# Mixed values, weight sums and weight splits re-ordered in the first, second and last u/gate group of a two-layer decoder trunk

## The chip, the cores and the metric

The kernel runs on one core of one Trainium2 chip, as one program. The metric is the device time of one execution in microseconds, the median of three timed runs. TensorE (PE in the profile) does the matrix products, VectorE (DVE) and ScalarE (ACT) work on what surrounds them, GpSimd (POOL) takes part of VectorE's kind of work, and SyncE (SP) issues the transfers between HBM and SBUF.

## The reference

One inference step of two layers on 1024 prompt tokens and 64 sample tokens, width 1024. Layer 0 is gated linear attention; layer 1, which the change touches, is a token-mixing MLP:

```python
def cmlp_mixer(h, w_in, ln_g, ln_b, w_spatial, b_spatial, w_out):
    u, v, gate = jnp.split(h @ w_in, 3, axis=-1)
    v = layernorm(v, ln_g, ln_b)
    ...
    mixed = jnp.einsum('gts,bnsgd->bntgd', ws, vg) + bs.T[:, :, None]
    z = u * mixed.reshape(bsz, t, CMLP_WIDTH) * jax.nn.silu(gate)
    return z @ w_out, v
```

Here `ws` is a 128x128 lower-triangular matrix for each of four groups of columns. A residual addition and a last RMSNorm follow. Everything is float32.

## The kernel before

**Arithmetic.** Each float32 operand of a product is written as a high part in the type float32r and a low part, the rest. A product is then three matmuls: high by high, high by low, low by high. Making the parts ("splitting") takes one ScalarE copy for the high part and one VectorE subtraction for the low part: `parts_of` (lines 969 to 974) and `fetch_w` (line 127 on ScalarE, line 128 on VectorE) for weights, `split` (lines 202 and 203) for activations.

**Stages.** Layer 0 comes first, then the projection to v (a block of 256 columns at a time, lines 1006 to 1050), then the u/gate stage that the change edits (the loop `for m in range(KT)`, eight groups m of 128 columns of u and 128 of gate), then the output projection `out_proj` with the weight blocks 28 to 31 (lines 790 to 862, matmuls at line 142).

**One u/gate group.** A group would be the product of a 256x1024 block of weights with 1088 tokens. It is done by a seven-product scheme of the Strassen kind on 2x2 quarters: seven quarter products (`product`, line 1004) with four sums of weight quarters, s1 to s4, three plain quarters, (1,1), (2,2) and (1,2), and sums of token quarters that were made beforehand (`tsum`). On TensorE a group is, in this order: the products with s2 (tile `pb`), s3 (`two`), s1 (`pb`), (1,1) (`p`); eight 128-column pairs of mixing matmuls (`mix`, line 1106); s4 (`pb`); the small mixing matmul of the 64 sample tokens (`mix`, line 1100); (2,2) (`two`); (1,2) (`p`). The mixing products go to two PSUM buffers (tag `o`). A chunk of four is taken out of its buffer by VectorE at line 1107, multiplied by a gain and added to `bias`, into `zt`; the small mixing matmul takes the first of the two buffers again, so it waits for the first instruction of line 1107.

**The weights of the next group.** `Quarters(blk)` loads a block's four pieces (256 KB each) into the single buffer `rawq` (line 964, on SyncE); `sums` makes s1 to s4 on GpSimd (line 985); `parts` splits a quarter or a sum (line 972 on ScalarE, 973 on VectorE) into a place whose old weights TensorE no longer needs. During group m the weights of group m+1 are summed and split, while `following` holds the load for group m+2, which can start when the last reader of `rawq` is done. The v rows of a group (`v_load`, tile `vm`) are loaded once the small mixing matmul of the group before has read them.

**Order.** The whole of the v and u/gate stages is written inside `in_order()`: on every engine the instructions run in the order of the code. An instruction that waits holds up everything behind it on its engine. After `order.close()` a scheduler chooses the order of the output projection again. The first group (m = 0) has its own placing of these steps, and so has the last (m = 7), since the operand `zs[0]` of the output projection (384 tokens of z: eight slices kt, of which 0 to 4 come through the tile `zstage`, 5 and 6 through two `zmore` tiles, 7 from `zt` directly) and the first weight block 28 (quarters 0 to 3, loaded by `load_w`, split by `fetch_w`) are split there.

**The tag `raw`.** The weight sums, the two `zmore` tiles and the loads of weight quarters take turns in three buffers; a load whose buffer still has a reader waits on SyncE, and so does all that is queued behind it there.

## Time and profile before

| | |
|---|---|
| timed runs | 940.91, 941.42, 944.12 us; median 941.42 us |
| the profiled execution | 944.72 us, of which 942.9 us from the first to the last instruction |
| mean granted TensorE clock | 0.991 |
| TensorE busy | 905.1 us, 96% of the span |
| VectorE, ScalarE, GpSimd busy | 640.8, 462.6, 285.4 us |
| u/gate groups m = 0 to 7 | from 637.71 us to 832.04 us of the span |
| output projection | from 832.04 us |

All places in time below are microseconds from the start of the span of this execution. A row of a timeline gives start, duration, engine, line, operation, output tile and input tiles, and how many instructions of one kind in a row it stands for; the bracket at its end is the idle time of the engine just before, and what ended it. A tile's name says which step a row belongs to: `wq` is a split weight, `qsum` a weight sum in a `raw` buffer, `qs` the sum s4, `half` a partial sum, `sg` the gate, `zt` the group's z, `act` the operand buffer, `wr` a loaded weight quarter of the blocks 28 to 31, `z` the later slices of the operand.

### The profile page before, as it was taken

The numbers are of one execution on the slowest core, as the hardware profiler recorded it, in microseconds if no ns is written. First come the engines' busy times: TensorE is split into PE (matmuls) and PEld (weight loads), VectorE is DVE, ScalarE is ACT, GpSimd is POOL, SyncE is SP. The second block draws the span as 40 slices with busy tenths as digits, with TensorE's granted clock in tenths as the row PEclk, the third lists the DMA queues.
The fourth block names the chain that finished last, engine by engine and source line by source line (L and its number), as shares of the span: only waits on it lengthen the run. The fifth ranks groups of instructions, "written<-read, shape, count | busy, mean of one in ns | idle before, by whom it ended". The sixth has DMA issues, their size and how long they took to land.

```text
span 942.9 us, 17092 instructions
## 1 busy us (share of the span) xinstructions
PE 905.1 (96%) x6437; PEld 880.3 (93%) x6437; DVE 640.8 (68%) x1288; ACT 462.6 (49%) x980; POOL 285.4 (30%) x307
## 2 busy tenths in 40 slices
PE   8989999999999999989999999999899999999995
PEld 8979989998999899978999999998899999999994
DVE  7888778677875877688553945556867777583246
ACT  7664544444462544554343644546444444455322
POOL 2023332232322331322133110023645555211123
PEclk9999999999999999999999999999989999999998
DMA  9302112311222112423574254463323332464133
GB/s 294 97 1 82 42 45 79 118 34 41 67 83 81 57 36 89 118 74 118 163 245 144 70 160 148 149 191 112 105 91 105 102 100 93 138 212 140 58 111 130
DMA packets 89967, 101.80 MB, mean 108 GB/s; under 512 B 9862, under 2 KB 80844, under 8 KB 89884
## 3 DMA queue, kind: packets, MB, share of 16 engines
q1 hardware_dynamic: 89884, 100.71, 34.0%
q8 instruction: 50, 0.82, 0.3%
q14 instruction: 33, 0.27, 0.1%
HBM read 74.26 MB, written 26.42 MB: 107 GB/s over the span
## 4 chain that ended last, share of the span: by engine, by line
PE 67%; DVE 14%; DMA 5%; issue 5%; ACT 5%; POOL 3%; SPq 1%; DVEq 0%; ACTq 0%; POOLq 0%
PE fm L142 28%; PE tm L156 12%; PE pb L1004 6%; PE two L1004 5%; PE p L1004 4%; DMA xsum<-x_spill 3%; PE sc L518 2%; PE pst L589 1%; PE o L628 1%; PE o L597 1%; DVE act L203 1%; DVE scT L531 1%; PE mix L1106 1%; PE first L285 1%; PE o L599 1%
## 5 line engine op out<-in xcount | busy, mean ns | idle before, releaser
L142 PE MATMUL fm<-act,w 128*128 128x384 f32 (+1 forms) x1632 | 290.2, 332 | 0.4 <-DVE act L203 0.4
L142 PEld LDWEIGHTS fm<-act,w 128*128 128x128 f32 x1632 | 269.8, 188 | 2.4 <-DVE act L203 0.6
L156 PE MATMUL tm<-w,act 128*128 128x256 f32 (+1 forms) x1536 | 192.6, 283 | 0.5 <-ACT vt L1015 0.5
L156 PEld LDWEIGHTS tm<-w,act 128*128 128x128 f32 x1536 | 185.4, 188 | 2.1 <-ACT vt L1015 0.7
L142 PE MATMUL fm<-act,wq 128*128 128x384 f32 (+1 forms) x576 | 96.6, 328 | 1.7 <-ACT wq L127 1.3
L142 PEld LDWEIGHTS fm<-act,wq 128*128 128x128 f32 x576 | 94.7, 188 | 3.2 <-ACT wq L127 1.6
L128 DVE TENSOR_TENSOR w<-wr,w 128x512 fp32r<-128x512 f32 (+1 forms) x80 | 57.3, 732 | 16.7 <-ACT w L127 16.1
L826 POOL TENSOR_TENSOR acc<-acc,sq 128x384 f32<-128x384 f32 (+1 forms) x30 | 31.0, 1037 | 110.0 <-ACT sq L821 109.5
L127 ACT ACTIVATE w<-wr 128x512 fp32r<-128x512 f32 (+1 forms) x80 | 48.7, 624 | 24.9 <-DMA wr<-w 13.2
L848 DVE TENSOR_TENSOR x<-fm,res 128x384 f32<-128x384 f32 (+1 forms) x40 | 21.0, 527 | 49.8 <-PE fm L142 49.8
L1004 PE MATMUL two<-tsum,wq 128*128 128x272 f32 x384 | 54.2, 299 | 0.1
L1004 PEld LDWEIGHTS two<-tsum,wq 128*128 128x128 f32 x384 | 51.7, 197 | 0.3 <-DVE wq L973 0.3
L821 ACT ACTIVATE sq<-x 128x384 f32<-128x384 f32 (+1 forms) x42 | 21.0, 503 | 62.1 <-DVE x L848 58.5
L1004 PE MATMUL pb<-act,wq 128*128 128x272 f32 x384 | 51.4, 290 | 0.0
L1004 PE MATMUL p<-act,wq 128*128 128x272 f32 x384 | 51.0, 288 | 0.0
L1004 PEld LDWEIGHTS p<-act,wq 128*128 128x128 f32 x384 | 49.4, 188 | 0.0
L1004 PEld LDWEIGHTS pb<-act,wq 128*128 128x128 f32 x384 | 49.0, 189 | 0.0
L473 POOL TENSOR_TENSOR xe<-xe,k 128x384 f32<-128x384 f32 (+2 forms) x24 | 28.7, 1197 | 44.2 <-ACT xe L472 41.1
L659 POOL TENSOR_TENSOR on<-on,g 128x384 f32<-128x384 f32 (+1 forms) x24 | 23.8, 1013 | 57.0 <-DVE on L658 34.2
L449 POOL TENSOR_TENSOR kd<-kd,k 128x384 f32<-128x384 f32 (+1 forms) x12 | 12.1, 1006 | 85.8 <-ACT kd L448 85.8
L973 DVE TENSOR_TENSOR wq<-qsum,wq 128x512 fp32r<-128x512 f32 x25 | 27.6, 1112 | 12.4 <-ACT wq L972 12.2
L480 DVE TENSOR_TENSOR xl<-cum 128x192 f32<-128x192 f32 (+4 forms) x72 | 35.1, 513 | 0.0
(265 smaller groups left out, 1641.8 us busy)
## 6 DMA issues: line engine op xcount, KB each, us to landing
wr<-w SPq DMA_DIRECT2D x92, 256.0 KB, 3.1
rawq<-w SPq DMA_DIRECT2D x32, 256.0 KB, 3.6
xsum<-x_spill SPq DMA_DIRECT2D x16, 272.0 KB, 3.3
z_spill<-zt SPq DMA_DIRECT2D x8, 544.0 KB, 2.8
s<-s SPq DMA_DIRECT2D x16, 256.0 KB, 3.9
state_s<-ns SPq DMA_DIRECT2D x32, 128.0 KB, 2.5
v_spill<-vt SPq DMA_DIRECT2D x32, 128.0 KB, 2.5
vm<-v_spill SPq DMA_DIRECT2D x8, 512.0 KB, 4.3
```

The source lines that it names most:

```text
L127: A.activation(w[:, 0], raw, AF.Copy)
L128: V.tensor_tensor(w[:, 1], raw, w[:, 0].bitcast(F32), ALU.subtract)
L142: PE.matmul(acc, lhs, rhs, start=(k == 0), stop=(k == 23))
L156: PE.matmul(acc, lhs, rhs, start=(k == 0), stop=(k == 23))
L473: G.tensor_tensor(xe, xe, kt_[:, :nl], ALU.mult)
L480: V.tensor_tensor(l3[:, :, lo:hi], c3[:, :, (i + 1) * m:], r, ALU.subtract)
L659: G.tensor_tensor(o, o, gate[h][:, j, t0:t0 + n], ALU.mult)
L821: A.activation(sq, raw[p][:, m, :], AF.Square)
L826: (V if gain is not None and p == 2 or m == KT - 1 else G).tensor_tensor(total, acc[p], sq, ALU.add)
L848: V.tensor_tensor(raw[p][:, m, :], pa, r, ALU.add)
L973: V.tensor_tensor(w[:, 1], src, w[:, 0].bitcast(F32), ALU.subtract)
L1004: PE.matmul(acc, lhs, rhs, start=start and k + i == 0, stop=k + i == 5, skip_group_check=not start)
```

## The change

Three places of the u/gate loop are written in another order; no work is added or left out. Line numbers move by up to 10 behind the first edit.

- First group (m = 0): the two line-1107 instructions go ahead of the three splits of plain quarters on VectorE; GpSimd makes the sums s3 and s4 right behind its four half-additions, ahead of its two multiplications into `zt`; the load of block 22 (`following`) is issued behind the three splits, ahead of the load of the next v rows on SyncE.
- Second group (m = 1): the two line-1107 instructions go ahead of the split of s3. In the groups 2 to 6 nothing changes.
- Last group (m = 7): slices 0 and 2 of the operand are split before the copies of the product with (1,1), slices 4 and 6 behind them; the loads of weight quarters 1 and 2 of block 28 are written sooner, quarter 1 is split behind the first SiLU instead of behind the second, quarter 2 behind the second; the two `zmore` buffers swap, so that the slice that is split first (6) holds the buffer that quarter 2 is loaded into.

The diff:

```diff
--- before.py
+++ after.py
@@ -1168,6 +1168,11 @@
             nxt.parts("s2", spare)
         if not more:
             fetch_w(28, [0])
+            load_w(28, 1)
+
+            zs = [act_all[:, :, :, lo:lo + n] for lo, n in zip((T - N, 0, N), size)]
+            for kt in (0, 2):
+                split(zs[0], kt, stage[:, kt, :])
         pa = [ps("mm", "p1")[:, :QUART] for r in R]
         for r in R:
             product(pa[r], w[1, 1], b11[r])
@@ -1186,25 +1191,28 @@
             G.tensor_tensor(p6[r], p6[r], p1[r], ALU.add)
             G.tensor_tensor(sg[:, qb[r]], sg[:, qb[r]], p1[r], ALU.add)
         if first:
+            nxt.sums("s3")
+            nxt.sums("s4", up)
+        elif not more:
+            split(zs[0], 4, stage[:, 4, :])
+            split(zs[0], 6, rest[0])
+            load_w(28, 2)
+        elif m > 1:
+            nxt.parts("s3", w[1, 1])
+        for c in range(2):
+            mixed(zt, vm, g, m, bias, 4 * c)
+        if m == 1:
+            nxt.parts("s3", w[1, 1])
+        if first:
             for key, at in (((1, 1), "s2"), ((2, 2), "s3"), ((1, 2), "s1")):
                 nxt.parts(key, w[at])
-        elif more:
-            nxt.parts("s3", w[1, 1])
-        else:
-
-            zs = [act_all[:, :, :, lo:lo + n] for lo, n in zip((T - N, 0, N), size)]
-            for kt in (0, 2, 4):
-                split(zs[0], kt, stage[:, kt, :])
-        for c in range(2):
-            mixed(zt, vm, g, m, bias, 4 * c)
+            following = Quarters(22)
         V.tensor_tensor(sg[:, fb], sg[:, fb], rs_all[:, fb], ALU.mult)
         A.activation(sg[:, fb], sg[:, fb], AF.Silu)
         if first:
             nxt.parts("s2", spare)
         if not more:
-            split(zs[0], 6, rest[1])
-            load_w(28, 1)
-            load_w(28, 2)
+            fetch_w(28, [1])
         for r in R:
             product(pb[r], w["s4"], b22[r], start=False)
             V.tensor_tensor(p1[r], p1[r], pb[r], ALU.add)
@@ -1215,18 +1223,14 @@
         V.tensor_tensor(sg[:, fb], sg[:, fb], rs_all[:, fb], ALU.mult)
         if more:
             vm = v_load(m + 1)
-        if first:
-            nxt.sums("s3")
-            nxt.sums("s4", up)
-            following = Quarters(22)
-        elif more:
+        if mid:
             nxt.parts("s1", w["s4"])
             if m + 2 == KT:
                 load_w(28, 0)
                 rest = [wp.tile([P, N], F32, tag="raw", bufs=3, name="zmore") for _ in range(2)]
-                SP.dma_start(rest[0], z_d[:, 5, 0:N])
-        else:
-            split(zs[0], 5, rest[0])
+                SP.dma_start(rest[1], z_d[:, 5, 0:N])
+        elif not more:
+            split(zs[0], 5, rest[1])
             load_w(28, 3)
             for kt in (1, 3):
                 split(zs[0], kt, stage[:, kt, :])
@@ -1242,13 +1246,11 @@
         V.tensor_tensor(sg[:, fa], sg[:, fa], rs_all[:, fa], ALU.mult)
         A.activation(sg[:, fa], sg[:, fa], AF.Silu)
         if not more:
-            fetch_w(28, [1])
+            fetch_w(28, [2])
         V.tensor_tensor(sg[:, fa], sg[:, fa], rs_all[:, fa], ALU.mult)
         for r in R:
             product(pa[r], w[1, 2], b21[r], start=False)
             V.tensor_tensor(zt[:, qa[r]], pa[r], zt[:, qa[r]], ALU.mult)
-        if not more:
-            fetch_w(28, [2])
         for part in ((slice(0, T),) if more else (slice(0, N), slice(N, T))):
             V.tensor_tensor(zt[:, part], zt[:, part], sg[:, part], ALU.mult)
             if not more:
@@ -1257,7 +1259,7 @@
         SP.dma_start(z_d[:, m, :], zt)
         if more:
             if m + 2 == KT:
-                SP.dma_start(rest[1], z_d[:, 6, 0:N])
+                SP.dma_start(rest[0], z_d[:, 6, 0:N])
             spare = w[1, 2]
             cur, nxt = nxt, following
         else:
```

**First group, VectorE.** The instructions of group 0 from the end of the product with s1 on, before (line 1107 is the mixed values, 973 the low part of a weight split):

```order
L1165 TENSOR_TENSOR sg<-sg,pb 128x272 x2
L973 TENSOR_TENSOR wq<-rawq,wq 128x512 x3
L1107 SCALAR_TENSOR_TENSOR zt<-mix,lng,bias 128x512 x2
L1200 TENSOR_TENSOR sg<-sg,rs 128x544
L973 TENSOR_TENSOR wq<-qsum,wq 128x512
L1210 TENSOR_TENSOR half<-half,pb 128x272 x2
L1101 SCALAR_TENSOR_TENSOR zt<-mix,lng,bias 128x64
L1215 TENSOR_TENSOR sg<-sg,rs 128x544
L1236 TENSOR_TENSOR sg<-half,two 128x272 x2
L973 TENSOR_TENSOR wq<-qsum,wq 128x512 x2
```

and in the changed kernel:

```order
L1165 TENSOR_TENSOR sg<-sg,pb 128x272 x2
L1107 SCALAR_TENSOR_TENSOR zt<-mix,lng,bias 128x512 x2
L973 TENSOR_TENSOR wq<-rawq,wq 128x512 x3
L1210 TENSOR_TENSOR sg<-sg,rs 128x544
L973 TENSOR_TENSOR wq<-qsum,wq 128x512
L1218 TENSOR_TENSOR half<-half,pb 128x272 x2
L1101 SCALAR_TENSOR_TENSOR zt<-mix,lng,bias 128x64
L1223 TENSOR_TENSOR sg<-sg,rs 128x544
L1240 TENSOR_TENSOR sg<-half,two 128x272 x2
L973 TENSOR_TENSOR wq<-qsum,wq 128x512 x2
```

The mixed values moved from behind the three splits of `rawq` quarters to ahead of them; behind the splits the order is the same. In the second group it is likewise the pair at line 1107 that now stands ahead of the last of that group's splits of sums before it.

**First group, GpSimd.** Before, from the sums s1 and s2 of block 21 on (line 985), past the half-additions (1186, 1187) and the multiplications into `zt` (1212, 1214), to the first sums of block 22:

```order
L985 TENSOR_TENSOR qsum<-qsum,rawq 128x512
L1186 TENSOR_TENSOR half<-half 128x272
L1187 TENSOR_TENSOR sg<-sg,half 128x272
L1186 TENSOR_TENSOR half<-half 128x272
L1187 TENSOR_TENSOR sg<-sg,half 128x272
L1212 TENSOR_TENSOR zt<-zt,half 128x272
L1214 TENSOR_TENSOR zt<-zt,half 128x272
L1075 MEMSET vm 64x128
L985 TENSOR_TENSOR qsum<-rawq 128x512
L985 TENSOR_TENSOR qs_7641<-rawq,qsum 128x512
L985 TENSOR_TENSOR qsum<-rawq 128x512
```

and in the changed kernel, where the half-additions are at 1191 and 1192 and the multiplications at 1220 and 1222:

```order
L985 TENSOR_TENSOR qsum<-qsum,rawq 128x512
L1191 TENSOR_TENSOR half<-half 128x272
L1192 TENSOR_TENSOR sg<-sg,half 128x272
L1191 TENSOR_TENSOR half<-half 128x272
L1192 TENSOR_TENSOR sg<-sg,half 128x272
L985 TENSOR_TENSOR qsum<-rawq 128x512
L985 TENSOR_TENSOR qs_7583<-rawq,qsum 128x512
L1220 TENSOR_TENSOR zt<-zt,half 128x272
L1222 TENSOR_TENSOR zt<-zt,half 128x272
L1075 MEMSET vm 64x128
L985 TENSOR_TENSOR qsum<-rawq 128x512
```

The sums s3 and s4 (`qs`) moved from behind the two multiplications and the clearing of `vm` to directly behind the half-additions.

**Start of the output projection, TensorE.** `fm_9657`, `fm_9691` and `fm_9727` are the first three output blocks; `wq_7366`, `wq_7468`, `wq_7471` and `wq_7292` are the quarters 0, 1, 2 and 3 of weight block 28. Before, from the second row of the stage to the first use of quarter 3:

```order
L142 MATMUL fm_9657<-act_80,wq_7468 128x384 x2
L142 MATMUL fm_9691<-act_80,wq_7366 128x384 x2
L142 MATMUL fm_9657<-act_80,wq_7468 128x384 x4
L142 MATMUL fm_9657<-act_80,wq_7471 128x384 x2
L142 MATMUL fm_9691<-act_80,wq_7366 128x384 x4
L142 MATMUL fm_9691<-act_80,wq_7468 128x384 x2
L142 MATMUL fm_9657<-act_80,wq_7471 128x384 x4
L142 MATMUL fm_9691<-act_80,wq_7468 128x384 x4
L142 MATMUL fm_9691<-act_80,wq_7471 128x384 x6
L142 MATMUL fm_9727<-act_80,wq_7366 128x384 x6
L142 MATMUL fm_9727<-act_80,wq_7468 128x384 x4
L142 MATMUL fm_9657<-act_80,wq_7292 128x384 x2
```

and in the changed kernel, from the first row of the stage:

```order
L142 MATMUL fm_9657<-act_80,wq_7366 128x384 x6
L142 MATMUL fm_9657<-act_80,wq_7468 128x384 x6
L142 MATMUL fm_9657<-act_80,wq_7471 128x384 x6
L142 MATMUL fm_9691<-act_80,wq_7366 128x384 x6
L142 MATMUL fm_9691<-act_80,wq_7468 128x384 x6
L142 MATMUL fm_9691<-act_80,wq_7471 128x384 x6
L142 MATMUL fm_9727<-act_80,wq_7366 128x384 x6
L142 MATMUL fm_9657<-act_80,wq_7292 128x384 x2
L142 MATMUL fm_9691<-act_80,wq_7292 128x384 x2
```

With the first row (6 matmuls) the kernel before has 46 matmuls ahead of the first one that needs quarter 3, the changed kernel 42.

**Last group, ScalarE.** From the second SiLU (line 1243) to the copy of quarter 3 of block 28, before:

```order
L1243 ACTIVATE sg_9330<-sg_9330 128x544
L127 ACTIVATE wq_7468<-wr28_1_9487 128x512
L127 ACTIVATE wq_7471<-wr28_2_9489 128x512
L202 ACTIVATE act_80<-z_9604 128x384 x4
L202 ACTIVATE act_80<-z_9614 128x384
L202 ACTIVATE act_80<-zt_9329 128x384
L202 ACTIVATE act_80<-z_9614 128x384 x2
L202 ACTIVATE act_80<-z_9622 128x320 x2
L202 ACTIVATE act_80<-zt_9329 128x384
L127 ACTIVATE wq_7292<-wr28_3_9525 128x512
```

and in the changed kernel, where that SiLU is at line 1247 and quarter 0 of block 29 (`wr29_0`) is a new row ahead of the slices `z`:

```order
L1247 ACTIVATE sg_9330<-sg_9330 128x544
L127 ACTIVATE wq_7471<-wr28_2_9475 128x512
L127 ACTIVATE wq_7331<-wr29_0_9685 128x512
L202 ACTIVATE act_80<-z_9604 128x384 x4
L202 ACTIVATE act_80<-zt_9329 128x384
L202 ACTIVATE act_80<-z_9614 128x384 x3
L202 ACTIVATE act_80<-z_9622 128x320
L202 ACTIVATE act_80<-zt_9329 128x384
L127 ACTIVATE wq_7292<-wr28_3_9527 128x512
```

Quarter 1 left this stretch (it is split in front of it, behind the first SiLU), quarter 0 of block 29 came in, and the copy of quarter 3 is still behind both `zt` slices.

## The prediction

> **What bounds the kernel now.** I read the page first: TensorE is busy 96% of the span, and the chain that ended last is mostly its matmuls, so an edit is worth what TensorE waits less. Then the list of TensorE's waits between 600 and 870 us (line waited for, total, times, longest):
>
> ```profile
> PE mix L1100 <- DVE zt L1107: 5.5, 2, 3.3
> PE fm L142 <- ACT wq L127: 1.3, 1, 1.3
> ```
>
> These are the three places that the change is written at. TensorE's timeline shows where they lie:
>
> ```profile
> 651.86 3.25 PE L1004 MATMUL pb<-act,wq 128*128 128x272 f32 x24
> 657.30 0.41 PE L1100 MATMUL mix<-wss,vm 128*128 128x64 f32 x2 [2.19 <-DVE zt L1107]
> ...
> 663.65 3.17 PE L1004 MATMUL pb<-tsum,wq 128*128 128x272 f32 x24
> ...
> 684.39 0.66 PE L1100 MATMUL mix<-wss,vm 128*128 128x64 f32 x2 [3.33 <-DVE zt L1107]
> 684.82 5.68 PE L1004 MATMUL two<-tsum,wq 128*128 128x272 f32 x24
> ...
> 710.21 0.33 PE L1100 MATMUL mix<-wss,vm 128*128 128x64 f32 x2
> 710.35 3.27 PE L1004 MATMUL two<-tsum,wq 128*128 128x272 f32 x24
> ...
> 832.04 1.22 PE L142 MATMUL fm<-act,wq 128*128 128x384 f32 x6
> 834.54 35.68 PE L142 MATMUL fm<-act,wq 128*128 128x384 f32 x211 [1.28 <-ACT wq L127]
> ```
>
> Group 2 (from 693.36, as the stretches below are cut) has no wait and needs 710.21 - 693.36 = 16.85 us to its small mixing matmul. Group 1 pays more than its 3.33: the row behind the gap takes 5.68 instead of 3.27, the small matmuls 0.66 instead of 0.33, 2.74 together. The stretches say why (last columns: granted clock, DMA share, GB/s):
>
> ```profile
> 663.65:693.36 29.71, 26.28 (x189) 25.88 (x187) 23.54 (x29) 12.15 (x27) 20.54 (x21) 0.89 0.34 112
> 693.36:716.47 23.11, 23.11 (x188) 23.11 (x187) 15.48 (x25) 10.92 (x24) 12.02 (x13) 1.00 0.31 100
> 656.00:658.00 2.00, 0.70 (x6) 0.73 (x7) 1.81 (x3) 0.00 (x0) 2.00 (x3) 1.00 0.00 0
> 689.00:690.00 1.00, 1.00 (x7) 1.00 (x6) 0.00 (x0) 0.00 (x0) 0.92 (x2) 0.50 0.00 0
> ```
>
> After the gap of 3.33 the clock is 0.50; in the gap of 2.19 it stayed 1.00. Whether every execution pays the 2.74 is open: of the timed runs, 940.91, 941.42 and 944.12, the slow one lies 2.7 above the median, and the profiled execution (944.72 = 942.9 of span and 1.8 around it) 3.3. I read this as two kinds of execution, and the median as one without the slow clock. The Trainium skill (TensorE: Matmul & The Clock Gate, Part 1) says that the gate looks at the array in free-running windows of about 3.4 us, so a gap just as long trips it in some runs only; the trace agrees as far as one execution can.
>
> **First group: the wait of 2.19.** VectorE's timeline:
>
> ```profile
> 652.41 4.08 DVE L973 TENSOR_TENSOR wq<-rawq,wq 128x512 fp32r<-128x512 f32 x3 [4.57 <-ACT wq L972]
> 656.42 1.40 DVE L1107 SCALAR_TENSOR_TENSOR zt<-mix,lng,bias 128x512 f32<-128x512 f32 x2
> 658.60 0.72 DVE L1200 TENSOR_TENSOR sg<-sg,rs 128x544 f32<-128x544 f32 x1 [0.79 <-POOL sg L1187]
> 660.57 0.69 DVE L973 TENSOR_TENSOR wq<-qsum,wq 128x512 fp32r<-128x512 f32 x1 [1.25 <-ACT wq L972]
> ```
>
> The mixing matmuls are issued by 651.86, yet line 1107 starts at 656.42, behind three splits. Put ahead, the pair (1.40) is over by about 653.5; TensorE wants its buffer at 651.86 + 3.25 = 655.1. The 2.19 goes, and TensorE reaches group 1 at 661.46 instead of 663.65. The splits end no later than before: VectorE idles from 657.8 to 658.6.
>
> **What the earlier sums cost.** What is late next is the split of s2 of the new weights, at 660.57 to 661.26, now needed at 661.46 (high part) and two matmuls later (low part). In front of it stands the multiplication at 658.60, which waits for GpSimd's last half-addition. GpSimd now goes straight on with s3 and s4:
>
> ```profile
> 657.79 0.77 POOL L1187 TENSOR_TENSOR sg<-sg,half 128x272 f32<-128x272 f32 x1
> 664.03 1.29 POOL L985 TENSOR_TENSOR qsum<-rawq 128x512 f32<-128x512 f32 x1
> 665.27 1.30 POOL L985 TENSOR_TENSOR qs<-rawq,qsum 128x512 f32<-128x512 f32 x1
> 671.61 1.97 POOL L985 TENSOR_TENSOR qsum<-rawq 128x512 f32<-128x512 f32 x1 [5.04 <-DMA rawq<-w]
> ```
>
> and VectorE beside such sums is slow: in group 2 a multiplication of the same shape takes 1.80,
>
> ```profile
> 715.85 1.80 DVE L1242 TENSOR_TENSOR sg<-sg,rs 128x544 f32<-128x544 f32 x1
> ```
>
> so it ends at 660.4 instead of 659.3, and SiLU, copy and split follow as before (660.57 + 0.69 is 1.94 behind 659.32): 662.3. TensorE has done two matmuls of 3.17 / 24 = 0.13 by 661.7 and waits 0.6. Bounds: 0, if VectorE gets in first, and 2.4, if both sums pass ahead of it.
>
> Then the load of block 22. It waits for s4, which read the single `rawq`; in the trace it was issued at 666.60 and its first sum began at 671.61, 5.0 later:
>
> ```profile
> 666.60 1.75 SPq L964 DMA_DIRECT2D rawq<-w  x4
> ```
>
> ```profile
> 669.55 0.67 ACT L1139 ACTIVATE half<-pb 128x272 f32<-128x272 f32 x2
> ```
>
> Now s4 ends at about 661.7, and the sums of block 22 can start at 666.7. That is good for group 1's weights, but VectorE is then at the last splits and the multiplication in front of the second SiLU; ScalarE holds the copies of line 1139 behind that SiLU, and TensorE's third product of group 1 cannot start without the first of them (begun at 669.55; TensorE, two products behind 663.65, was there at about 670). Arriving two us sooner, TensorE meets it: between 0.15, if VectorE passes first, and 1.35, if it waits for a sum; I take 0.75. The v rows, now queued on SyncE behind the load of block 22, are issued at about 663.5 instead of 657.7; they are needed at about 669, and I cost them at nothing.
>
> **Second group: the wait of 3.33.** VectorE's row and, from the chain that ended last, its second half:
>
> ```profile
> 678.90 4.68 DVE L973 TENSOR_TENSOR wq<-qsum,wq 128x512 fp32r<-128x512 f32 x2
> 683.51 1.40 DVE L1107 SCALAR_TENSOR_TENSOR zt<-mix,lng,bias 128x512 f32<-128x512 f32 x2
> ```
>
> ```profile
> 679.77 3.82 DVE wq L973
> ```
>
> The split that takes 3.82 moves behind the mixed values. Then the first instruction of line 1107 can run at 679.77 and end at 680.5, if VectorE's other work stands where it stood: it gains the start that is about one us sooner, and loses about as much to five instructions that now meet the sums of block 22. TensorE, at 661.46 + 0.6 + 0.75 + 16.85 = 679.7, waits less than one us, and the small matmul comes at 680.4 instead of 684.39: **4.0 gained** in the two groups together. Ends: 6.1 (TensorE never waits: 661.46 + 16.85 = 678.3) and 2.3 (below). A gap under one us is shorter than the 2.19 that left the clock alone, so the 2.74 goes too, where it was paid.
>
> The Trainium skill (SBUF — State Buffer, Who interferes with whom) says that a VectorE instruction with two SBUF inputs and a GpSimd instruction that reads SBUF exclude each other for a whole instruction, and that one with a single SBUF input is left alone. That speaks against sums made sooner, and for moving line 1107, which reads PSUM: its pair takes 1.40 beside GpSimd at 656.42 as alone. By this rule no wait is longer than one GpSimd instruction, line 1107 would be through at 679.8, the two groups would gain about 4.6 and the forecast be 937.7; the 3.82 is longer than any single one in these rows, so I keep the wider end.
>
> **Last group: the wait of 1.28.** ScalarE and VectorE at the start of the output projection, SyncE's loads of z, and the chain:
>
> ```profile
> 833.88 1.14 ACT L127 ACTIVATE wq<-wr 128x512 fp32r<-128x512 f32 x2
> 836.24 2.33 ACT L202 ACTIVATE act<-z 128x384 fp32r<-128x384 f32 x5 [1.23 <-DMA z<-z_spill]
> 840.89 0.62 ACT L127 ACTIVATE wq<-wr 128x512 fp32r<-128x512 f32 x1
> 841.70 0.68 DVE L128 TENSOR_TENSOR wq<-wr,wq 128x512 fp32r<-128x512 f32 x1
> 831.51 1.68 SPq L1276 DMA_DIRECT2D z<-z_spill  x3
> 834.54 67.53 PE fm L142 x402
> ```
>
> Quarter 1 is split behind the first SiLU instead of at 833.88, and the wait at 833.26 goes. But TensorE then runs into quarter 3. At 67.53 / 402 = 0.168 per matmul, the 42 matmuls that now stand ahead of it are over at 832.04 + 7.1 = 839.1. Its copy on ScalarE comes behind ten copies of z and zt, and these wait for a transfer (836.24), issued at 831.51. The earlier quarters do not bring that forward: a 256 KB load (quarter 0 of block 29) is new in front of it, and the split that frees the buffer of quarter 3, which stands ahead on SyncE, is only some 0.5 sooner. So the copy ends at about 841.5 as before, and VectorE's half, with one more split (0.5) ahead of it, at 843.0 instead of 842.4. TensorE waits two us at 839.3. Before, it had done 51 matmuls at 842.4; now 49 at 843.0: 0.6 + 2 x 0.168, **0.9 lost**. Bounds: 1.28 gained, if the z transfer lands sooner by as much, and 1.3 lost.
>
> **The sum.** Profiled execution: 944.72 - 4.0 - 2.74 + 0.9 = 938.9. Median, which I take to lack the 2.74: 941.42 - 4.0 + 0.9 = **938.3**.
>
> **Rivals.**
> - *The median paid for the slow clock too* (0.2): then 2.74 more goes: 935.6. For it: the one profiled execution had it. Against: the spread of the timed runs.
> - *GpSimd keeps VectorE out for its whole chain* (0.2): as in the row of 3.82, now at the two splits ahead of line 1107. GpSimd's four half-additions end at about 680.2, two splits and line 1107 follow, the small matmul comes at 682.1: 2.3 gained, 940.0.
> - *The last group does what its edit says* (0.1): no wait at quarter 3: 941.42 - 4.0 - 1.28 = 936.1. Against: the transfer at 836.24.
> - *Slower* (0.05): the same chain in group 1, but pushed on further by the later half-additions, so that line 1107 is not ahead of 684 again; then nothing is gained, the gap is long enough to halve the clock in every execution, and 941.42 + 2.74 + 0.9 = 945.1. It decides from a first line 1107 that ends behind 684. Against: the 3.82 itself has left the queue in front.
>
> **How the numbers follow.** The forecast has 0.45, with 936.5 to 940.0 from its own bounds. 0.3% of 941.42, about what a measurement of this kernel tells from no change, is 2.8, so 938.6 divides: of the forecast rather more than half lies under it. Faster 0.25 + 0.2 + 0.1 = 0.55; within 0.20 + 0.2 = 0.40; slower 0.05. The range takes in the first three rivals: 934.8 to 940.9.
>
> **What would show it.** Right: no wait of line 1100 in group 0, one under 1.5 us in group 1, clock 1.00 throughout groups 0 to 2; new short waits at the first products of group 1 (line 1004 on wq, on `half`); the 1.28 at quarter 1 gone and a wait of about two us on line 127 near 839. Wrong: a wait of over 3 us left at line 1100, or no wait at quarter 3.

## The result, and the profile after

| | before | changed |
|---|---|---|
| median of 15 runs each | 943.50 us | 937.03 us |
| lowest to highest | 939.75 to 944.88 | 934.22 to 940.01 |
| ratio, 95% interval | | 0.9935 (0.9920 to 0.9949) |
| the profiled execution, its span | 944.72, 942.9 | 939.36, 937.6 |
| group 0 starts | 637.71 | 639.60 |
| groups 0 and 1 | 55.65 | 48.20 |
| groups 2 to 7 | 138.68 | 138.68 |
| first matmul of the output projection to the end | 110.86 | 111.12 |

Faster by 0.65%, 6.5 us; the forecast was 938.3 with 934.8 to 940.9. As a ratio to its own 941.42 the forecast was 0.9967, outside the measured interval. The median of before is 943.5 once there are 15 runs of it; the 941.42 that the prediction started from came from three. The spans differ by 5.3: 7.45 gained in groups 0 and 1, 0.26 lost behind, and 1.89 lost ahead of group 0, where the two programs are the same. The granted clock falls there at one place in each profile, after at 420 to 430 us and before at 10 to 20 us (PE, PEld, DVE, ACT, POOL busy, then the clock, DMA share and GB/s). After:

```profile
420.00:430.00 10.00, 9.98 (x48) 9.41 (x49) 7.25 (x19) 7.01 (x12) 1.70 (x2) 0.83 0.17 54
```

Before:

```profile
10.00:20.00 10.00, 9.89 (x47) 9.81 (x48) 9.81 (x18) 10.00 (x23) 2.14 (x3) 0.83 1.08 349
```

Ten us at 0.83 are 1.7 us of matmuls lost in either. At 420 to 430 the changed kernel's execution falls back by 1.6 us: VectorE's instruction at line 371 comes at 397.97 where it came at 399.13 before, the one at line 459 at 424.98 where it came at 424.58. The other 1.5 of its lag come between there and group 0, at a clock of 1.00, and their cause stays open. Group 0 starts between 635.31 and 640.01 us in the fourteen profiles of these kernels, which are the same up to there; so stages are compared below by their own lengths, not by their places in the span.

TensorE's waits between 600 and 870 us, after:

```profile
PE pb L1004 <- DVE half L1218: 1.3, 1, 1.3
PE fm L142 <- ACT wq L127: 0.8, 1, 0.8
```

Line 1100 is gone from the list. TensorE's timeline at the places that the prediction quotes, after:

```profile
653.75 3.26 PE L1004 MATMUL pb<-act,wq 128*128 128x272 f32 x24
656.85 0.33 PE L1100 MATMUL mix<-wss,vm 128*128 128x64 f32 x2
...
664.61 3.26 PE L1004 MATMUL pb<-tsum,wq 128*128 128x272 f32 x24 [1.35 <-DVE half L1218]
...
670.72 3.16 PE L1004 MATMUL pb<-act,wq 128*128 128x272 f32 x24
...
681.54 0.33 PE L1100 MATMUL mix<-wss,vm 128*128 128x64 f32 x2
681.68 3.27 PE L1004 MATMUL two<-tsum,wq 128*128 128x272 f32 x24
...
826.48 8.13 PE L142 MATMUL fm<-act,wq 128*128 128x384 f32 x42
835.37 14.91 PE L142 MATMUL fm<-act,wq 128*128 128x384 f32 x89 [0.76 <-ACT wq L127]
```

Neither small mixing matmul waits, the product behind the second takes 3.27 and not 5.68, and group 1 is 23.19 us long where group 2 is 23.12:

```profile
639.60:664.61 25.01, 23.67 (x188) 23.23 (x187) 15.70 (x31) 15.83 (x35) 11.08 (x12) 1.00 0.27 82
664.61:687.80 23.19, 23.19 (x186) 23.19 (x187) 21.70 (x33) 10.70 (x25) 18.29 (x18) 1.00 0.53 166
```

What is left of group 0's loss is the 1.35 in front of group 1. VectorE and GpSimd, after:

```profile
653.14 1.65 DVE L1107 SCALAR_TENSOR_TENSOR zt<-mix,lng,bias 128x512 f32<-128x512 f32 x2 [3.40 <-DMA rawq<-w]
654.70 3.56 DVE L973 TENSOR_TENSOR wq<-rawq,wq 128x512 fp32r<-128x512 f32 x3
660.39 1.79 DVE L1210 TENSOR_TENSOR sg<-sg,rs 128x544 f32<-128x544 f32 x1 [2.13 <-POOL sg L1192]
663.43 0.69 DVE L973 TENSOR_TENSOR wq<-qsum,wq 128x512 fp32r<-128x512 f32 x1 [1.25 <-ACT wq L972]
664.04 0.78 DVE L1218 TENSOR_TENSOR half<-half,pb 128x272 f32<-128x272 f32 x2
...
668.32 0.71 DVE L1246 TENSOR_TENSOR sg<-sg,rs 128x544 f32<-128x544 f32 x1
...
679.37 1.40 DVE L1107 SCALAR_TENSOR_TENSOR zt<-mix,lng,bias 128x512 f32<-128x512 f32 x2
```

```profile
660.32 1.27 POOL L985 TENSOR_TENSOR qsum<-rawq 128x512 f32<-128x512 f32 x1
...
669.08 1.30 POOL L985 TENSOR_TENSOR qsum<-rawq 128x512 f32<-128x512 f32 x1 [2.29 <-DVE sg L1246]
```

The multiplication at line 1210 runs beside the sooner sum s3 and takes 1.79; behind it come SiLU, the split of s2 and then line 1218, whose two additions free TensorE's accumulators `pb`. The load of block 22 is issued on SyncE 663.37 - 639.60 = 23.8 us behind the start of group 0, in the kernel before 666.60 - 637.71 = 28.9 us behind it:

```profile
663.37 1.75 SPq L964 DMA_DIRECT2D rawq<-w  x4
```

Its sums begin 29.5 us behind the start of group 0 instead of 33.9, and line 1107 of group 1 starts 39.8 us behind it (679.37) instead of 45.8: its first half (0.7) is done 1.5 us before TensorE is there.

### The profile page after: what moved, and what is told of

It is laid out like the page before. It is cut to its first block, busy times and chain, and to the rows that moved or that the text cites. A ratio compares the mean times of both kernels' runs of the same rounds, so it can differ in the third digit from the quotient of the medians.

```text
span 937.6 us, 17096 instructions
## 1 busy us (share of the span) xinstructions
PE 904.3 (96%) x6437; PEld 877.5 (94%) x6437; DVE 638.7 (68%) x1288; ACT 461.4 (49%) x980; POOL 287.1 (31%) x307
## 4 chain that ended last, share of the span: by engine, by line
PE 66%; DVE 15%; ACT 5%; DMA 5%; issue 5%; POOL 2%; SPq 1%; DVEq 0%; ACTq 0%; POOLq 0%
PE fm L142 27%; PE tm L156 12%; PE pb L1004 7%; PE two L1004 5%; PE p L1004 4%; DMA xsum<-x_spill 2%; PE sc L518 2%; PE mix L1106 1%; PE pst L589 1%; PE o L628 1%; PE o L597 1%; DVE scT L531 1%; DMA wr<-w 1%; PE o L599 1%; PE tms L172 1%
## 5 line engine op out<-in xcount | busy, mean ns | idle before, releaser
L1004 PE MATMUL two<-tsum,wq 128*128 128x272 f32 x384 | 51.5, 290 | 0.0
L1004 PEld LDWEIGHTS two<-tsum,wq 128*128 128x128 f32 x384 | 49.2, 189 | 0.0
L659 POOL TENSOR_TENSOR on<-on,g 128x384 f32<-128x384 f32 (+1 forms) x24 | 23.8, 1015 | 57.9 <-DVE on L658 35.1
L483 DVE TENSOR_TENSOR xl<-xl,q 128x192 f32<-128x192 f32 (+4 forms) x72 | 28.9, 439 | 4.8 <-ACT xl L481 4.8
```

The source lines that it names most:

```text
L483: V.tensor_tensor(l3[:, :, lo:hi], l3[:, :, lo:hi], q3[:, :, (i + 1) * m:], ALU.mult)
L659: G.tensor_tensor(o, o, gate[h][:, j, t0:t0 + n], ALU.mult)
L1004: PE.matmul(acc, lhs, rhs, start=start and k + i == 0, stop=k + i == 5, skip_group_check=not start)
```

## The experiments

My theory: the gain has three parts, namely the mixed values ahead of the splits in group 0, the sooner load of block 22, without which group 1 gives the first part back, and the clock that no longer falls; the last group brings nothing. Rivals: each listed wait was worth its length; the median did not pay for the clock; the sooner sums only cost. In all the runs below the ratio is to the kernel before on the same chip, with five rounds of timings.

**The mixed values of group 0 alone.** In the kernel before, the two calls of `mixed` of the first group move ahead of its three splits:

```diff
-        if first:
-            for key, at in (((1, 1), "s2"), ((2, 2), "s3"), ((1, 2), "s1")):
-                nxt.parts(key, w[at])
...
         for c in range(2):
             mixed(zt, vm, g, m, bias, 4 * c)
+        if first:
+            for key, at in (((1, 1), "s2"), ((2, 2), "s3"), ((1, 2), "s1")):
+                nxt.parts(key, w[at])
```

> Only the two mixed values of the first group go ahead of its three splits. The two groups m = 0 and 1 took 55.65 us in the kernel before (first product of group 0 to first product of group 2) and 48.20 in the changed one. Account on record, by its steps: the wait of 2.19 goes, but block 22 arrives as late as before, so the mixed values of group 1 still end at about 684, TensorE comes there two us sooner and waits about 5 us instead of 3.33, with the slow clock behind it: 55.2 to 55.9, the time as before. Rival, each wait is worth its own length: 53.5, and 2.2 us faster.

Measured: ratio 1.0008 (0.9989 to 1.0028), the two groups 55.55 us. Its TensorE:

```profile
655.91 0.33 PE L1100 MATMUL mix<-wss,vm 128*128 128x64 f32 x2
...
662.62 3.25 PE L1004 MATMUL pb<-tsum,wq 128*128 128x272 f32 x24 [0.28 <-DVE half L1210]
666.87 0.52 PE L1004 MATMUL two<-tsum,wq 128*128 128x272 f32 x2 [1.01 <-ACT wq L972]
668.00 3.03 PE L1004 MATMUL two<-tsum,wq 128*128 128x272 f32 x22 [0.61 <-DVE wq L973]
...
685.20 0.66 PE L1100 MATMUL mix<-wss,vm 128*128 128x64 f32 x2 [3.30 <-DVE zt L1107]
```

The 2.19 is gone, 1.90 of it comes back as three waits at the start of group 1 (0.28 for line 1210, which reads the accumulators `pb`, 1.62 for weights), and the 3.30 stands as before. This listed wait was worth nothing by itself.

**The mixed values of group 1 alone**, with the same exchange for m = 1:

```diff
-        elif more:
+        if mid and m > 1:
             nxt.parts("s3", w[1, 1])
...
         for c in range(2):
             mixed(zt, vm, g, m, bias, 4 * c)
+        if m == 1:
+            nxt.parts("s3", w[1, 1])
```

> Only the two mixed values of the second group go ahead of the split of s3. Account on record: the split of 3.82 leaves the queue in front of them, the first one ends at about 680.4 while TensorE arrives at 681.1, no wait there and no slow clock: the two groups take 55.65 - 3.33 - 2.74 = 49.6 us, and the time falls by about 6 in executions with the slow clock, by 3.3 in others. Rival, GpSimd keeps VectorE out until its four half-additions end at 683: a wait of over 2 us is left, 52 us or more.

Measured: 0.9950 (0.9930 to 0.9969), the two groups 50.44 us. The split that moved behind takes 2.54 there, out of TensorE's way. But a wait of group 0 that had left the clock alone in the kernel before trips it in this execution:

```profile
658.98 0.41 PE L1100 MATMUL mix<-wss,vm 128*128 128x64 f32 x2 [2.11 <-DVE zt L1107]
659.19 4.78 PE L1004 MATMUL two<-tsum,wq 128*128 128x272 f32 x24
```

The stretch behind the gap has a granted clock of 0.50:

```profile
660.00:661.00 1.00, 1.00 (x6) 1.00 (x6) 0.73 (x1) 0.00 (x0) 0.24 (x1) 0.50 0.42 123
```

4.78 instead of 3.27 for 24 matmuls: without that the two groups would be about 48.9 us, if group 1 then stays as it is. The wait of 3.33 is gone here without any sooner load.

**All of the first group's edits alone** (mixed values, sooner sums, sooner load):

```diff
         if first:
-            for key, at in (((1, 1), "s2"), ((2, 2), "s3"), ((1, 2), "s1")):
-                nxt.parts(key, w[at])
...
+            nxt.sums("s3")
+            nxt.sums("s4", up)
...
         for c in range(2):
             mixed(zt, vm, g, m, bias, 4 * c)
+        if first:
+            for key, at in (((1, 1), "s2"), ((2, 2), "s3"), ((1, 2), "s1")):
+                nxt.parts(key, w[at])
+        if first:
+            following = Quarters(22)
...
-        if first:
-            nxt.sums("s3")
-            nxt.sums("s4", up)
-            following = Quarters(22)
```

> All edits of the first group (mixed values ahead, sums s3 and s4 sooner, load of block 22 sooner), none of the second and the last. Theory 1, the earlier load of block 22 is what lets group 1's VectorE work end in time: in the changed kernel its mixed values were ready 1.5 us ahead of TensorE, and the split of s3 in front of them would cost about 1.3, so the wait at the small matmul is under 1 us, the clock stays, the two groups take 48.2 to 49.2. Theory 2, the edit of the second group is what removes the wait of 3.33: the split is kept out by GpSimd again, a wait of over 2 us is left, 51 us or more.

Measured: 0.9941 (0.9921 to 0.9961), the two groups 48.51 us; the small mixing matmul of group 1 waits 0.27, with line 1107 still behind the split. So the first group's edits bring nearly all of it (48.20 with everything), and the second group's edit, where they stand, 0.3.

**The changed kernel with the sums and the load at their old places:**

```diff
-        if first:
-            nxt.sums("s3")
-            nxt.sums("s4", up)
...
-            following = Quarters(22)
...
+        if first:
+            nxt.sums("s3")
+            nxt.sums("s4", up)
+            following = Quarters(22)
         if mid:
             nxt.parts("s1", w["s4"])
```

> The changed kernel with GpSimd's sums s3 and s4 of block 21 and the load of block 22 back at their old places (behind the two multiplications into zt); the mixed values stay ahead of the splits in both groups. My theory: the load of block 22 starts 3 us later again, so group 1's weights come later, its first products wait again (about 1.9 us in all as with the first group's mixed values alone), line 1107 of group 1 starts about 1.5 us after TensorE wants it; the 1.35 at the start of group 1 goes, since the multiplication is no longer beside a sum. The two groups take about 50.4 us (48.20 in the changed kernel, 55.65 before), timed about 939.2. Rival: the sooner sums only cost (the 1.35 in front of group 1) and the moved mixed values bring the rest: then the two groups take 48.20 - 1.35 = 46.9 us, timed about 935.7.

Measured: 0.9959 (0.9944 to 0.9973), the two groups 51.05 us. TensorE:

```profile
661.52 3.25 PE L1004 MATMUL pb<-tsum,wq 128*128 128x272 f32 x24 [0.52 <-DVE half L1214]
665.77 0.52 PE L1004 MATMUL two<-tsum,wq 128*128 128x272 f32 x2 [1.00 <-ACT wq L972]
666.89 4.56 PE L1004 MATMUL two<-tsum,wq 128*128 128x272 f32 x22 [0.61 <-DVE wq L973]
```

Both sides of the sooner sums show: without them the wait in front of group 1 is 0.52 and not 1.35, and 1.61 stand in its place at the next product, whose weights are late. Behind these waits the clock is 0.50 from 668 to 671 us: 22 matmuls take 4.56, where 22 behind the same waits took 3.03 in the run with the mixed values of group 0 alone. The rival (46.9) falls.

The runs so far, by which edits of the first two groups they have:

| mixed values of group 0 | sums and load sooner | mixed values of group 1 | groups 0 and 1, us |
|---|---|---|---|
| | | | 55.65 |
| moved | | | 55.55 |
| | | moved | 50.44 |
| moved | | moved | 51.05 |
| moved | yes | | 48.51 |
| moved | yes | moved | 48.20 |

So the wait of 3.33 and the slow clock behind it have two cures, and either is enough: the mixed values of group 1 ahead of the split, or the sooner sums and load. Once one is there the other adds less, 2.9 for the sums and 0.3 for the exchange. Moving the mixed values of group 0 brings nothing without the sooner sums. Sums and load were not moved apart from each other, nor without that exchange. Each row is one profile; the timings of the last four kernels (ratios 0.9935 to 0.9959, intervals from 0.9920 to 0.9973) can't put them in order.

**The split of s2 sooner.** In the changed kernel, `nxt.parts("s2", spare)` of the first group ahead of the multiplication:

```diff
             following = Quarters(22)
+            nxt.parts("s2", spare)
         V.tensor_tensor(sg[:, fb], sg[:, fb], rs_all[:, fb], ALU.mult)
         A.activation(sg[:, fb], sg[:, fb], AF.Silu)
-        if first:
-            nxt.parts("s2", spare)
```

> The changed kernel with the split of s2 of block 21 in the first group moved ahead of the multiplication of the gate on VectorE (and ahead of the SiLU on ScalarE), right behind the three splits of plain quarters. Its sum was ready at 656.5 in the changed kernel, so the split should run at 658.3 and not at 663.4, and the two additions of line 1218 that free TensorE's accumulators follow the multiplication at once (662.2 instead of 664.0). My theory: the wait of 1.35 in front of group 1 goes altogether, TensorE reaches group 1 at 23.7 us behind the start of group 0 instead of 25.0; the load of block 22 is unchanged, so part of it may come back as a wait inside group 1: the two groups take 46.9 to 47.6 us (48.20 in the changed kernel), timed about 936. Rival: the wait moves on to the third product of group 1, which needs ScalarE's copies behind the second SiLU, or to the splits of group 1's weights, and nothing is gained (48.2).

Measured: 0.9956 (0.9935 to 0.9977), the two groups 50.99 us: neither. TensorE reaches group 1 after 23.99 us as expected, but then:

```profile
661.90 3.25 PE L1004 MATMUL pb<-tsum,wq 128*128 128x272 f32 x24 [0.32 <-DVE half L1217]
...
681.05 0.41 PE L1100 MATMUL mix<-wss,vm 128*128 128x64 f32 x2 [2.03 <-DVE zt L1107]
681.27 4.76 PE L1004 MATMUL two<-tsum,wq 128*128 128x272 f32 x24
```

```profile
683.00:684.00 1.00, 1.00 (x6) 1.00 (x5) 1.00 (x4) 1.00 (x2) 0.77 (x2) 0.50 0.63 211
```

VectorE ahead of line 1107, and GpSimd beside it (four half-additions with no gap, 676.16 to 679.09):

```profile
675.97 3.68 DVE L973 TENSOR_TENSOR wq<-rawq,wq 128x512 fp32r<-128x512 f32 x1
679.57 0.68 DVE L973 TENSOR_TENSOR wq<-qsum,wq 128x512 fp32r<-128x512 f32 x1
```

```profile
676.16 0.76 POOL L1191 TENSOR_TENSOR half<-half 128x272 f32<-128x272 f32 x1
...
678.33 0.76 POOL L1192 TENSOR_TENSOR sg<-sg,half 128x272 f32<-128x272 f32 x1
```

A split of 0.68 took 3.68 and ended at 679.65, 0.56 behind the chain: the prediction's rival "GpSimd keeps VectorE out for its whole chain", which the changed kernel itself escapes. In the kernel before, the split of 3.82 ended at 683.59, 0.55 behind the last of the same four (683.04). Since s2 was split by 658.2 and the 0.32 still ended with line 1217, what TensorE waits for at the start of group 1 are the accumulators, not the weight.

**The same, with the mixed values of group 1 ahead of that split too:**

```diff
-        if mid:
+        if m > 1 and more:
             nxt.parts((1, 2), w["s1"])
             nxt.parts("s2", spare)
...
         if m == 1:
+            nxt.parts((1, 2), w["s1"])
+            following = Quarters(23)
+            nxt.parts("s2", spare)
             nxt.parts("s3", w[1, 1])
```

> The changed kernel with the split of s2 sooner in the first group (as in the run before) and, in the second group, the mixed values ahead of three splits instead of one: also ahead of those of quarter (1,2) and of s2, on VectorE and ScalarE; the load of block 23 stands behind the split of (1,2). In the run with s2 alone sooner, TensorE reached group 1 after 23.99 us (25.01 in the changed kernel), but there a split of (1,2) took 3.68 us beside GpSimd's four half-additions and held up the mixed values: a wait of 2.03, and the clock fell. My theory: that split is the cause; with the mixed values ahead of it the small mixing matmul does not wait, and the two groups take 23.99 + 23.1 = 47.1 us (48.20 in the changed kernel, 50.99 with s2 alone), timed about 936. Rival: the three splits behind now stand ahead of the multiplication in front of the first SiLU and of line 1218, which frees TensorE's accumulators, and of GpSimd's chain: TensorE waits about as long (1 to 2 us) at the start of group 2, and nothing is gained over the changed kernel (48.2 or more).

Measured: 0.9927 (0.9911 to 0.9942), the two groups 47.55 us. Its waits between 600 and 870 us:

```profile
PE fm L142 <- ACT wq L127: 0.7, 1, 0.7
...
PE pb L1004 <- DVE half L1220: 0.4, 1, 0.4
```

Line 1100 is off the list, so the wait of 2.03 came from the splits that stood ahead of line 1107; 0.40 stand in front of group 1. 0.65 us better than the changed kernel in the profile, which the timings (0.9935, 0.9920 to 0.9949) can't tell apart.

**The last group's edits alone**, in the kernel before (the diff is the last group's part of the one above):

> Only the edits of the last group. From the first matmul of the output projection to the last instruction: 110.9 us in the kernel before, 111.1 in the changed one. Account on record: the wait of 1.28 at quarter 1 is gone, TensorE waits for quarter 2's low half and for quarter 3 instead; 111.1 to 111.8, the time as before within 1 us. Rival, the 1.28 is gained: 109.6, 1.3 us faster.

Measured: 1.0011 (0.9991 to 1.0031), from the output projection's first matmul to the end 111.12 us.

```profile
832.78 8.15 PE L142 MATMUL fm<-act,wq 128*128 128x384 f32 x42
841.67 8.56 PE L142 MATMUL fm<-act,wq 128*128 128x384 f32 x47 [0.73 <-ACT wq L127]
```

The wait moved from quarter 1 to quarter 3, as in the changed kernel: nothing gained.

**Quarter 3 sooner**, in the changed kernel:

```diff
-            fetch_w(28, [2])
+            fetch_w(28, [2, 3])
...
-        else:
-            fetch_w(28, [3])
```

> The changed kernel with quarter 3 of block 28 split right behind quarter 2, ahead of the copies of the slices of z and zt on ScalarE and VectorE. My theory: the wait of 0.76 at quarter 3 goes, and the 0.3 to 1 us that TensorE waited unseen among the 42 matmuls before it stays: from the first matmul of the output projection to the end 110.3 us (111.12 in the changed kernel, 110.86 before); timed about 936.3. Rival: the copies of zt come 0.6 us later, TensorE waits at slice 7 of the operand instead, and nothing is gained (111.1).

Measured: 0.9935 (0.9913 to 0.9956), 111.19 us: the rival. TensorE waits 0.94 for a copy of line 202, slice 7:

```profile
824.21 6.25 PE L142 MATMUL fm<-act,wq 128*128 128x384 f32 x31
831.39 13.88 PE L142 MATMUL fm<-act,wq 128*128 128x384 f32 x81 [0.94 <-ACT act L202]
```

**Quarters 2 and 3 sooner:**

```diff
         V.tensor_tensor(sg[:, fa], sg[:, fa], rs_all[:, fa], ALU.mult)
-        A.activation(sg[:, fa], sg[:, fa], AF.Silu)
         if not more:
             fetch_w(28, [2])
+        A.activation(sg[:, fa], sg[:, fa], AF.Silu)
...
+        if not more:
+            fetch_w(28, [3])
         for part in ((slice(0, T),) if more else (slice(0, N), slice(N, T))):
...
-        else:
-            fetch_w(28, [3])
```

> The changed kernel with quarter 2 of block 28 split ahead of the second SiLU on ScalarE (its low part directly behind the multiplication in front of that SiLU, where VectorE waits anyway), and quarter 3 split ahead of the last multiplications of zt. My theory: at the start of the output projection TensorE loses not the 0.76 of the listed wait alone but 8.89 - 42 x 0.168 = 1.83, since the 42 matmuls ahead of it also wait for quarter 2; with both quarters sooner and the slices of zt about one us sooner nearly all of it goes: from the first matmul of the output projection to the end 109.3 us (111.12 in the changed kernel, 110.86 before, 111.19 with quarter 3 alone), timed about 935.4. Rival: slice 7 or a slice that comes by the z transfer is next, as slice 7 was with quarter 3 alone: 110.5 to 111.1.

Measured: 0.9931 (0.9916 to 0.9946), 111.02 us.

```profile
823.28 3.65 PE L142 MATMUL fm<-act,wq 128*128 128x384 f32 x20
827.09 0.44 PE L142 MATMUL fm<-act,wq 128*128 128x384 f32 x1 [0.16 <-DVE wq L128]
828.62 16.67 PE L142 MATMUL fm<-act,wq 128*128 128x384 f32 x98 [1.09 <-ACT act L202]
```

Again the wait only changed its name, and again the stage is as long. VectorE, on which the slices of zt depend, is busy 14.01 of the 16 us from 813 to 829 here:

```profile
813.00:829.00 16.00, 14.75 (x108) 14.18 (x107) 14.01 (x25) 7.13 (x16) 3.75 (x4) 1.00 0.53 174
```

So no order of the weights' splits alone made this stage shorter. That VectorE's load is what bounds it was not tried by taking work from it.

**Filling the gap**, to price the clock by itself: the kernel before with extra 128x128 matmuls in group 1, in front of the small mixing matmul. They start the sums in the banks of `two` anew, so that group 1's z lacks its product with s3.

```diff
+        if m == 1:
+            for i in range(24):
+                PE.matmul(two[:, i % 2, QUART:QUART + P], ws[:, g, :], ws[:, g, :], start=True, stop=True)
         mixed(zt, vm, g, m, bias, 0, True)
```

> The kernel before, in its old order, with 24 extra 128x128 matmuls of ws by ws in the second u/gate group, ahead of the small mixing matmul; their results are used by nothing. They fill TensorE's idle 3.3 us there (16 such matmuls took 1.95 us, so 24 take about 2.9 at full clock). My theory: half of what the second group lost was not the wait but the slow clock behind it; with the gap filled the small mixing matmul still comes at the same distance (20.7 us) behind the start of the group, but the clock stays 1.00, the product behind it takes 3.3 instead of 5.7 us, the two groups take 55.65 - 2.74 = 52.9 us, and the timed ratio is about 0.997 (941.0 against 943.8). Rival: the median run did not pay for the slow clock, as the prediction had it: no change in the timed median (ratio 1.000), whatever the one profiled execution shows.

Measured: 1.0017 (1.0000 to 1.0034). I had the price of the filler wrong, since such a matmul leaves two records: 24 took 5.52 us, 2 more than the gap. A second version with 13 of them in the banks of `pb`:

```diff
+                PE.matmul(pbf[i % 2][:, QUART:QUART + P], ws[:, g, :], ws[:, g, :], start=True, stop=True)
```

> The kernel before, in its old order, with 13 extra 128x128 matmuls of ws by ws in the second u/gate group, ahead of the small mixing matmul, into unused columns of the banks of pb; nothing reads them. In the run with 24 such matmuls they took 5.52 us, 2 us more than the idle time that they were to fill, and so showed the clock but not its price; 13 take 5.52 x 13 / 24 = 3.0 us of the 3.33. My theory: the wait itself stays, the clock stays 1.00 and the two groups take 55.65 - 2.74 = 52.9 us; timed 0.997 (941.5 against 944.2), with a mean granted clock over the runs of about 0.994, where the kernel before has 0.991 to 0.992. Rival: most executions of the kernel before do not pay for the clock at this place: timed 1.000.

Measured: 1.0060 (1.0041 to 1.0080). It failed as a test: the matmuls had to wait until line 1211 had read these banks, so they came behind the gap instead of into it:

```profile
685.78 5.46 PE L1216 MATMUL pb<-ws 128*128 128x128 f32 x26 [4.88 <-DVE half L1211]
```

The third has 12, in the banks of `two` again:

> The kernel before with 12 extra 128x128 matmuls of ws by ws at the place of the run with 24 of them (into the banks of two, where they started at once behind the product with s4; they start the sums in these banks anew, so that group 1's z lacks its product with s3). 24 took 5.52 us, so 12 take 2.8 of the idle 3.3. My theory: most executions of the kernel before pay for the slow clock behind this gap. Then the clock stays 1.00 here, the small mixing matmul comes no later, the two groups take 55.65 - 2.74 = 52.9 us, the mean granted clock over the runs is about 0.994 where the kernel before has 0.991 to 0.992, and the timed ratio is about 0.997. Rival: most executions do not pay: the clocks and times of the two kernels are alike, ratio 1.000.

Measured: 0.9982 (0.9968 to 0.9997), the two groups 52.30 us.

```profile
677.77 2.84 PE L1215 MATMUL two<-ws 128*128 128x128 f32 x24
681.28 0.41 PE L1100 MATMUL mix<-wss,vm 128*128 128x64 f32 x2 [0.67 <-DVE zt L1107]
681.50 3.26 PE L1004 MATMUL two<-tsum,wq 128*128 128x272 f32 x24
```

The small mixing matmul comes no sooner behind the start of the group than before (20.78 and 20.74 us), the product behind it takes 3.26 and not 5.68, and the kernel is faster by 1.8 us for doing more work. (The two groups are 0.6 shorter than the 52.9 expected because the wait of group 0 happens to be 1.44 in this profile, where it was 2.19.) The other half of the test is the mean granted clock that each timed execution reports. Time lost to it, span x (1 - clock), is a rough figure, since the clock is given to three places (0.001 is 0.94 us), so only means over the runs stand here:

| kernel | runs | mean clock | lost, us | span x clock, us |
|---|---|---|---|---|
| before, beside the experiments | 92 | 0.9915 | 8.0 | 934.2 |
| before, beside the last filler alone | 17 | 0.9910 | 8.5 | 933.6 |
| last filler (12) | 12 | 0.9938 | 5.8 | 934.4 |
| mixed values of group 0 alone | 12 | 0.9909 | 8.6 | 933.9 |
| last group alone | 12 | 0.9914 | 8.1 | 934.3 |
| first group alone | 12 | 0.9941 | 5.5 | 930.4 |
| changed | 15 | 0.9947 | 5.0 | 930.2 |

The three kernels with the gap of 3.3 lose 8 us to the clock, those without it 5 to 6, the filler 2.7 less than before beside it (1.3 to 4.0 by the spread of the runs). The others fit: the remaining kernels without that gap, the filler of 24 among them, lose 4.7 to 6.4, the one of 13, with its gap of 4.88, 9.6. So the profile's 2.74 is what the executions pay on average and most of them pay it; the rival of no change falls. The timed gain is less, 1.8, since the filler's span x clock is 0.8 longer.

## Why the prediction was right or wrong

**The waits of 2.19 and 3.33** went, the first by the step given. For the second the prediction has one step, the split of 3.82 that leaves the queue in front of line 1107; it is enough by itself (50.44), but so are the first group's edits with that split left in front (48.51). The two groups gained 7.45 in the profile, 2.74 of it the clock and 4.7 the rest; forecast 4.0, bounds 2.3 and 6.1.

**"TensorE has done two matmuls of 3.17 / 24 = 0.13 by 661.7 and waits 0.6"**: 1.35. The account of the path (multiplication beside s3 in 1.79, forecast 1.80; SiLU, copy, split) was right: the split of s2 is done at 664.12, 0.86 behind the 663.26 at which TensorE is free, and less the two matmuls that is the 0.6. The end of the path was not: the wait ends one instruction of VectorE's queue later, at line 1218, as the run with s2 sooner shows.

**"between 0.15, if VectorE passes first, and 1.35"** at the third product of group 1, taken at 0.75: nothing. VectorE passed first; GpSimd's first sum of block 22 waited for the multiplication at 668.32. TensorE, later by the other wait, was at the third product at 670.72 and found the copies done. The two terms add up to 1.35 in the forecast and 1.35 in the profile; that is luck, since both were wrong.

**Line 1107 of group 1 "at 679.77"**, which is 42.1 us behind the start of group 0: 39.8. VectorE's other work was to gain one us by the sooner sums of block 22 and lose as much; the sums began 4.4 sooner, and 2.3 of that were left at line 1107. So TensorE, forecast to wait 0.7 there, does not meet it, and by these rows would not have met it if it had come the whole 1.35 sooner. In the run with s2 sooner it was line 1107 that came late, 42.3 us behind the start of group 0, because of the split of 3.68; TensorE, a us earlier at group 1, waited 2.03 there.

**Last group, 0.9 lost**: right in kind, 0.26 in the profile. Quarter 3's copy ended at 835.32, 8.8 us behind the start of the stage, where 9.5 were forecast; 42 x 0.168 = 7.06 of the 8.89 us up to there are matmuls, so 0.76 is the listed wait and 1.07 lie among the matmuls before it.

**"Median, which I take to lack the 2.74"** is the step that failed. Three times, the highest 2.7 above the median, were read as two kinds of execution, and the one profile as the slow kind. Most executions pay, as the filled gap and the mean clocks show; the clock also falls at other places, which differ from one execution to the next. The right sum is 943.5 - 4.7 - 2.74 + 0.3 = 936.4 against the 937.03 measured. The forecast of 938.3 came near by luck, because the base was 2.1 too low and the gain 3.4 too small; the rival that the median paid for the clock is what happened.

**The clock and the two rules.** The gap of 3.3 halved the clock in each of its three profiles, 2.11 and 2.03 did so in one each (rows of 0.50), and 2.19 did not. The Trainium skill (TensorE: Matmul & The Clock Gate, Part 1) names an idle window of about 3.4 us; the traces disagree as far as these two shorter gaps tripped it. The rule of the Trainium skill (SBUF — State Buffer, Who interferes with whom), that the two exclude each other for a whole instruction, was read as a limit of one GpSimd instruction on the wait and so gave 937.7, nearer to the result than the forecast, yet for the wrong reason: the 3.68 and the 3.82, each beside four GpSimd instructions, stand against that reading.

## What to carry to other kernels

A wait in the list is worth its length only if what is late next is no later: here the wait of 2.19 taken out alone was worth nothing (1.0008), because weights and line 1107 were late next, while the one of 3.33 went by either of two edits, so that their gains do not add up. Before a wait is priced, look at the rows behind it for a changed matmul time, and take the mean clock over many executions before saying that a median lacks it. Where several placings of the same steps give the same stage (110.9 to 111.2 four times), stop moving them.

## What the hardware showed that I had not expected

- A gap of TensorE under 3 us can halve its clock: 2.03 and 2.11 did, for 1.5 us over the next 24 matmuls; so did three waits of 0.52, 1.00 and 0.61 within 6 us (22 matmuls in 4.56), while one of 2.19 did not, nor did 0.28, 1.01 and 0.61 in a row (22 in 3.03).
- The same program loses between 0.4% and 1.3% of its span to the clock from one execution to the next (0.996 to 0.987 in 92 runs of the kernel before); one place of it, at 420 to 430 us in layer 0, set the profile after back by 1.6 us.
- VectorE was kept out by a chain of GpSimd instructions, not by one: 3.68 and 3.82 for a split that takes 0.68, both ending 0.55 or 0.56 behind the chain. In the changed kernel a split beside the same four took 1.25; what decides between the two is not shown.
